# Softmax row sums in a two-layer hybrid trunk: one running sum with a split, or four partial sums in four quarters of the array

## The chip, the cores and the metric

The kernel runs on one core of one Trainium2 chip. The metric is the time of one execution on the device in microseconds (us). The program is one launch. TensorE (PE) multiplies, VectorE (DVE), ScalarE (ACT) and GpSimd (POOL) do the elementwise work, SyncE (SP) issues every DMA. Each engine takes its instructions in its own order and waits at an instruction until what it needs is there.

## The reference, cut to what matters

Two layers. Each has grouped-query attention and a gated linear recurrence side by side on the same normalised input. 1024 latent tokens and 256 context tokens; 16 query heads share 4 key heads of width 64. The part that matters here is the softmax:

```python
def gqa(q, k, v):
    s = jnp.einsum('bqkgd,bskd->bkgqs', q, k).astype(jnp.float32)
    p = jax.nn.softmax(s, axis=-1).astype(v.dtype)
    return jnp.einsum('bkgqs,bskd->bqkgd', p, v)
...
        o_lat = latent_attention(q_l, k_all, v_all)
...
        x = x + gt_l * merge_branches(o_lat, ga_l, lru_l, gb_l, gm_l, w_a_out[l], w_b_out[l], w_out[l])
```

Latent queries see 1280 keys (256 context, 1024 latent), context queries (first layer only) see the 256 context keys. All arithmetic is fp32 in the reference.

## The kernel before, in words

Features lie on the partitions, tokens on the free axis. To keep fp32 accuracy at the fast rate, the kernel writes an operand as a high and a low part in the type fp32r and adds three products (high·high, high·low, low·high).

A layer runs in four stages: queries, keys and values (line 709); the recurrence (766); attention, with the projections of the gates beside it (908); the output projections (1114). The change is in the third.

**Attention.** `Unit` (line 942) is 512 query columns of one head against ten tiles of 128 keys. A pair of heads has four units; in the first layer a fifth one (`e == 2`) takes the 256 context queries of both heads against two key tiles. The first layer has 32 full and 8 context units, the second 32 full ones. What a unit does, in the order of time:

- `load` (964): three DMAs bring the queries; POOL clears the lower half of `qb`.
- `s1` (977): twelve products give scores of 128 queries against up to 512 keys, and DVE takes their maxima into `mp`. `smax` and `aug` (984, 989): DVE reduces these to one maximum per query in column 64 of `mz`, PE transposes four 128x65 blocks, and ACT writes the negative maxima into row 64 of `qb`, so that the next product subtracts them.
- `s2` (996), for each key tile: two products give the shifted scores with keys on the partitions. ACT takes the exponential twice, as fp32 (`pf`) and as fp32r (`ph`). DVE subtracts: `pl` is the rest, pf − ph. `add` (1011): POOL adds `pf` to the running sum `acc`, nine additions for ten tiles.
- `av` (1020): two products with the values, one for `ph` and one for `pl`. `evac` (1028) brings the result out.
- `lparts` (1040): POOL copies `acc` to an fp32r tile `ah`, DVE subtracts to get the rest `al`. `lsum` (1046): two products with a column of ones add the 128 partitions of both into one row, ACT copies the row out, and a DMA writes it to memory.
- `recip` (1059), once for the two heads: a DMA brings the sums back as 128 partitions by 8, DVE takes reciprocals, a DMA writes them, two DMAs spread them over the partitions, and `done` (1080) scales the output.

**Order.** The class `Timeline` (63) keeps a clock of its own: each product adds a planned cost (`mm`, 135), and everything else is put into a list with a due time. The products of the gates' projections (`fills`, 901) fill the time between, and before each the due work is emitted. Within attention the due times are in steps of one key tile (lines 947 to 962), stretched by `pace` (1105), which is worked out from the planned costs. The order on PE is as emitted; the other engines' order is made from the emission by the tile framework. Tiles come from rings: three buffers of `pf`, two of `acc`, six PSUM banks for all scores and sums.

Of the kernel before, what the change touches and what calls it, by code (L numbers as in the profile page):

```python
# [62 lines left out]
class Timeline:  # L63
    """Orders the emission by the tensor engine's clock: products fill, other work is due at times."""
# [36 lines left out]
def trunk_kernel(ctx: ExitStack, tc: tile.TileContext, xT, cc, par, wmod, win, wgate, wo,  # L101
# [47 lines left out]
    # ---------------------------------------------------------------- constants  # L149
# [17 lines left out]
    ones_r = const.tile([128, 1], F32R, name="onesr")  # L167
    V.tensor_copy(ones_r, ones)
# [11 lines left out]
    # silu of the two conditions  # L180
# [10 lines left out]
    # 4 * softplus(-lam), by log1p(z) = 2 atanh(z / (2 + z)), z = exp(-|lam|)  # L191
# [27 lines left out]
    # ---------------------------------------------------------------- weights  # L219
# [53 lines left out]
    def w_next():  # L273
        """the next weight tile; the one after it is being made ready"""
# [26 lines left out]
    # ---------------------------------------------------------------- modulation  # L301
# [19 lines left out]
    def modulation(l, i, b, half, wm, box):  # L321
        """four feature tiles' part of 512 columns of shift | scale | gate, on the tensor engine"""
# [9 lines left out]
    def mod_turn(l, i, n, ps, wait):  # L332
        """two rows of sums to features on the partitions"""
# [12 lines left out]
    def modulation_side(l, blocks, work):  # L346
        """the same, its products beside the tensor engine"""
# [29 lines left out]
    # ---------------------------------------------------------------- hidden state  # L377
# [8 lines left out]
    def sq_add(work, c, j, x):  # L386
        """adds the squares of feature tile j of x"""
# [9 lines left out]
    def rsqrt_small(ss, scale, t):  # L397
        """t[:, 0] = 1 / sqrt(ss * scale + eps), with one Newton step"""
# [7 lines left out]
    def norm_chunk(l, c, xs, gap):  # L406
        """events that make the hidden state's two parts from xs [128, 8, n] and its squares"""
# [35 lines left out]
    # ---------------------------------------------------------------- queries and keys  # L443
# [8 lines left out]
    class Group:  # L452
        """two column tiles of queries or keys: product, per-head norm, rotation, two parts"""
# [22 lines left out]
        def sums(self, i, c, hi, lo):  # L476
            """sums of squares of the tile's two heads, in rows"""
# [12 lines left out]
        def norm(self, i):  # L490
            """their reciprocal roots, spread over all partitions"""
# [53 lines left out]
    def layer_dram(l):  # L545
# [7 lines left out]
        d["l"] = {(t, c): dtile(l, f"l{t}{c}", [2, 2, CH[c][1]]) for t in range(8) for c in och}  # L553
# [17 lines left out]
    def first_products(g):  # L571
        """the first group's products, with the last chunk of tokens last"""
# [11 lines left out]
    # ---------------------------------------------------------------- start  # L584
# [19 lines left out]
    with tc.tile_pool(name="prep", bufs=1, reuse_waits="tile") as work:  # L604
# [16 lines left out]
        def scale_rows(c):  # L621
            """x times the reciprocal root of its mean square, in its place"""
# [34 lines left out]
        def modulate(c, k0, nk=4):  # L657
            """the hidden state's two parts"""
# [44 lines left out]
    # ---------------------------------------------------------------- layers  # L703
    for l in range(DEPTH):
# [4 lines left out]
        # ---------------- queries, keys, values  # L709
# [169 lines left out]
            # the first of the gate projections cover the last scans  # L879
# [28 lines left out]
        # ---------------- attention, with the projections of the gates beside it  # L908
        use_banks("g")
        weng[0] = "a"  # L910
        with tc.tile_pool(name="att", bufs=2, reuse_waits="tile") as work:
            kv = {}

            def load_kv(g):
# [6 lines left out]
                G.memset(r32(k2[64:128]), 0.0)  # L921
# [4 lines left out]

            mzs = []
            for i in range(3):
# [160 lines left out]
            for t in range(8):  # L1089
                if t % 2 == 0:  # L1090
                    add(g0 - 19 if t else -25, lambda t=t: load_kv(t // 2))
                for c, e in [("L0", 0), ("L0", 1), ("L1", 0), ("L1", 1)] + ([] if last else [("C", 2)]):
# [5 lines left out]
                    if e:  # L1098
                        cost += 0.864 * CH[c][1] / 512
# [229 lines left out]
```

## Time and profile before

| | us |
|---|---|
| median of three runs (lowest, highest) | 3306.36 (3296.35, 3307.05) |
| span of the profiled execution, first to last instruction | 3297.0 |
| PE busy in the span | 3059.3 (93%) |
| DVE busy | 2656.1 (81%) |
| ACT busy | 1789.4 (54%) |
| POOL busy | 1435.6 (44%) |
| attention of the first layer, the stretch read below | 640 to 1380 |
| attention of the second layer, the stretch read below | 2340 to 3010 |

Of the profiled execution the page gives the span alone, so every sum is made against 3297.0; the median lies 9.4 us above it, and what a sum gives as a difference is applied to the median. Busy shares are averages over stages with different limits, so each stage has to be read by itself. A product's duration in the trace includes the time in which its results leave the array, and the next product starts before that: the distance of two starts tells the rate, not the duration.

### The profile page before, as it was taken

The numbers are of one execution on the slowest core, as the hardware profiler recorded it, in microseconds if no ns is written. First come the engines' busy times: TensorE is split into PE (matmuls) and PEld (weight loads), VectorE is DVE, ScalarE is ACT, GpSimd is POOL, SyncE is SP. The second block draws the span as 40 slices with busy tenths as digits, with TensorE's granted clock in tenths as the row PEclk, the third lists the DMA queues.
The fourth block names the chain that finished last, engine by engine and source line by source line (L and its number), as shares of the span: only waits on it lengthen the run. The fifth ranks groups of instructions, "written<-read, shape, count | busy, mean of one in ns | idle before, by whom it ended". The sixth has DMA issues, their size and how long they took to land.

```text
span 3297.0 us, 42932 instructions
## 1 busy us (share of the span) xinstructions
PE 3059.3 (93%) x14392; PEld 2437.3 (74%) x14392; DVE 2656.1 (81%) x3696; ACT 1789.4 (54%) x3140; POOL 1435.6 (44%) x1119
## 2 busy tenths in 40 slices
PE   7999999999989999999899999998998988899999
PEld 3778788777767677787777788776766666677887
DVE  7874887699999999766685876896899999997544
ACT  5433667366666666545655435665566666664222
POOL 0111443366667666435522212443577766773000
PEclk9999999999999999999999999999999999999999
DMA  5442111312112111264554451113212121114554
GB/s 196 145 162 91 48 50 63 112 52 69 59 61 78 54 58 61 86 196 154 177 198 157 144 179 48 52 48 94 83 50 60 54 71 52 52 53 139 195 177 138
DMA packets 218654, 331.14 MB, mean 100 GB/s; under 512 B 39184, under 2 KB 84904, under 8 KB 218176
## 3 DMA queue, kind: packets, MB, share of 16 engines
q1 hardware_dynamic: 218432, 328.39, 30.7%
q8 instruction: 113, 1.85, 0.2%
q14 instruction: 109, 0.89, 0.1%
HBM read 252.13 MB, written 76.17 MB: 100 GB/s over the span
## 4 chain that ended last, share of the span: by engine, by line
PE 43%; DVE 34%; issue 8%; POOL 6%; ACT 4%; DMA 4%; SPq 1%; DVEq 0%; POOLq 0%; ACTq 0%
PE gps L143 25%; DVE pl L1007 9%; DVE mp L982 6%; PE s2ps L143 4%; DVE wlo L227 4%; PE avps L143 4%; PE s1ps L143 2%; PE qps L143 2%; PE vps L143 2%; PE gtps L143 1%; DVE ti L851 1%; POOL macc L360 1%; POOL acc L1018 1%; POOL b L848 1%; DVE z L1085 1%
## 5 line engine op out<-in xcount | busy, mean ns | idle before, releaser
L143 PE MATMUL gps<-h,whi 128*128 128x512 f32 x3328 | 1042.7, 395 | 19.8 <-DVE g L871 14.5
L1018 POOL TENSOR_TENSOR acc<-acc,pf 128x512 f32<-128x512 f32 x512 | 745.4, 1456 | 339.9 <-ACT pf L1005 319.0
L1007 DVE TENSOR_TENSOR pl<-pf,ph 128x512 fp32r<-128x512 f32 x656 | 753.1, 1150 | 12.7 <-ACT ph L1006 10.3
L143 PEld LDWEIGHTS gps<-h,whi 128*128 128x128 f32 x3328 | 609.1, 189 | 145.4 <-issue 9.3
L143 PE MATMUL gps<-h,wlo 128*128 128x512 f32 x1664 | 654.5, 393 | 1.4 <-DVE wlo L227 1.4
L1005 ACT ACTIVATE pf<-s2ps 128x512 f32<-128x512 f32 x656 | 392.2, 598 | 382.4 <-issue 164.2
L982 DVE TENSOR_REDUCE mp<-s1ps 128x1 f32<-128x512 f32 (+1 forms) x800 | 450.5, 581 | 44.8 <-PE s1ps L143 43.5
L227 DVE TENSOR_TENSOR wlo<-wraw,whi 128x512 fp32r<-128x512 f32 x392 | 348.0, 910 | 80.6 <-POOL whi L224 43.1
L1006 ACT ACTIVATE ph<-s2ps 128x512 fp32r<-128x512 f32 x656 | 389.0, 593 | 0.0
L143 PEld LDWEIGHTS gps<-h,wlo 128*128 128x128 f32 x1664 | 314.8, 189 | 71.3 <-DVE wlo L227 2.1
L226 ACT ACTIVATE whi<-wraw 128x512 fp32r<-128x512 f32 x324 | 193.8, 628 | 304.4 <-PE gps L143 261.5
L143 PE MATMUL s1ps<-k,qa 128*128 128x512 f32 (+1 forms) x800 | 291.2, 372 | 58.1 <-DVE mp L982 37.1
L143 PE MATMUL avps<-pl,vv 128*128 128x512 f32 x656 | 266.7, 407 | 24.6 <-DVE pl L1007 23.0
L143 PE MATMUL s2ps<-qa,k 128*128 128x512 f32 x656 | 264.5, 403 | 18.2 <-DVE mp L982 15.9
L360 POOL TENSOR_TENSOR macc<-macc,wmt 128x512 f32<-128x512 f32 x112 | 155.8, 1391 | 250.9 <-ACT wmt L358 227.8
L143 PE MATMUL s2ps<-qb,k 128*128 128x512 f32 x656 | 259.5, 396 | 0.0
L143 PE MATMUL avps<-ph,vv 128*128 128x512 f32 x656 | 259.1, 395 | 0.0
L143 PE MATMUL gps<-e,whi 128*128 128x512 f32 x768 | 243.9, 399 | 0.2 <-DVE e L227 0.2
L143 PEld LDWEIGHTS s1ps<-k,qa 128*128 128x128 f32 x800 | 151.3, 190 | 116.4 <-DVE mp L982 63.4
L143 PE MATMUL qps<-h,whi 128*128 128x512 f32 x640 | 204.6, 401 | 1.7 <-DVE h L669 0.9
L143 PE MATMUL gps<-c,whi 128*128 128x256 f32 x1024 | 197.9, 288 | 2.3 <-DVE c L222 2.0
L527 POOL TENSOR_TENSOR t<-qg,rc 128x512 f32<-128x512 f32 x40 | 57.6, 1439 | 322.7 <-DVE qf L532 161.4
(225 smaller groups left out, 5325.0 us busy)
## 6 DMA issues: line engine op xcount, KB each, us to landing
wraw<-in_win_dram SPq DMA_DIRECT2D x200, 256.0 KB
wraw<-in_wo_dram SPq DMA_DIRECT2D x192, 256.0 KB
wm<-in_wmod_dram SPq DMA_DIRECT2D x32, 512.0 KB
wm<-in_wmod_dram SPq DMA_DIRECT2D x8, 1024.0 KB
rb<-rq SPq DMA_DIRECT2D x64, 128.0 KB
k<-k SPq DMA_DIRECT2D x24, 320.0 KB
v<-vst SPq DMA_DIRECT2D x20, 256.0 KB
vv<-v SPq DMA_DIRECT2D x8, 640.0 KB
```

The source lines that it names most:

```text
L143: nc.tensor.matmul(o, a, b, start=start, stop=stop)
L226: S.activation(dst_hi, src, AF.Copy)
L227: (V if lo_eng == "v" else G).tensor_sub(dst_lo, src, r32(dst_hi))
L360: G.tensor_add(acc, acc, t)
L527: G.tensor_mul(t1, a, rc[:, o:o + n])
L848: G.tensor_mul(a2, a2, ti)
L851: V.tensor_tensor_scan(h, a, a2, 0.0, op0=OP.mult, op1=OP.add)
L982: tl.at(0.3, lambda: V.reduce_max(self.mp[:, j, b:b + 1], ps[:, :n], axis=AX.X))
L1005: S.activation(pf, ps, AF.Exp)
L1006: S.activation(ph, ps, AF.Exp)
L1007: tl.at(1.4, lambda: V.tensor_sub(pl, pf, r32(ph)))
L1018: G.tensor_add(self.acc, self.acc, pf)
```

## The change

Four things change, all in attention.

1. The sums. A full unit keeps four partial sums, of the key tiles (0, 1, 2), (3, 4, 5), (6, 7) and (8, 9), a context unit two of one tile each. `lparts` goes: no `ah`, no `al`. `lsum` multiplies each partial sum, as it is in fp32, with a 128x32 block of ones, and each result goes to its own 32 partitions of one PSUM bank, so that each product stands in its own quarter of the array's columns. The plan counts 0.9 us for all of them.
2. The way back. The four rows of sums go to memory, `recip` brings them back with a DMA for each head, DVE adds the four and takes the reciprocal.
3. The maxima. `mz` is a 128x4 tile without the 64 cleared columns, the transposes put one row out each, and the second product of `s2` takes 65 rows instead of 128, so that `qb` and `k2` need no clearing.
4. The plan: `lsum` is due at 3.6 instead of 4.0 (5.0 instead of 6.0 for a context unit), `pace` follows the new costs. Comments and docstrings are taken out, so line numbers differ.

```diff
-    def mm(o, a, b, start, stop):
+    def mm(o, a, b, start, stop, cost=None):
...
-        if b.dtype == F32R:
+        if cost is not None:
+            tl.now += cost
+        elif b.dtype == F32R:
...
+    ones32 = const.tile([128, 32], F32, name="ones32")
+    V.memset(ones32, 1.0)
...
-                    add(g0 + self.nkt + (4.0 if e == 2 else 2.0), self.lparts)
-                    add(g0 + self.nkt + (6.0 if e == 2 else 4.0), self.lsum)
+                    add(g0 + self.nkt + (5.0 if e == 2 else 3.6), self.lsum)
+                    self.groups = ((0,), (1,)) if e == 2 else ((0, 1, 2), (3, 4, 5), (6, 7), (8, 9))
+                    self.accs = {}
...
-                    G.memset(r32(qb[64:128]), 0.0)
...
-                        tr(pt[0:65, j * 128:(j + 1) * 128], mz[:, j, :])
-                    S.activation(self.qb[64:65], pt[64:65, :], AF.Copy, scale=-1.0)
+                        tr(pt[0:1, j * 128:(j + 1) * 128], self.mz[:, j:j + 1])
+                    S.activation(self.qb[64:65], pt[0:1, :], AF.Copy, scale=-1.0)
...
-                    mm(ps, k2[:, ks], self.qb, False, True)
+                    mm(ps, k2[0:65, ks], self.qb[0:65], False, True)
...
                 def add(self, kt, pf):
-                    if kt == 0:
-                        self.first = pf
-                        self.acc = work.tile([128, 512], F32, name="acc", tag="acc", bufs=2)
-                    elif kt == 1:
-                        G.tensor_add(self.acc, self.first, pf)
+
+                    x = next(x for x, g in enumerate(self.groups) if kt in g)
+                    at = self.groups[x].index(kt)
+                    if at == 0:
+                        self.accs[x] = pf
+                        if self.e == 2:
+                            G.tensor_scalar(self.acc_tile(x), pf, 1.0, 0.0, op0=OP.mult, op1=OP.add)
+                    elif at == 1:
+                        first = self.accs[x]
+                        G.tensor_add(self.acc_tile(x), first, pf)
                     else:
-                        G.tensor_add(self.acc, self.acc, pf)
+                        G.tensor_add(self.accs[x], self.accs[x], pf)
+
+                def acc_tile(self, x):
+                    self.accs[x] = work.tile([128, 512], F32, name="acc", tag="acc", bufs=5)
+                    return self.accs[x]
...
-                def lparts(self):
-                    self.ah = work.tile([128, 512], F32R, name="ah", tag="ah", bufs=1)
-                    self.al = work.tile([128, 512], F32R, name="al", tag="al", bufs=1)
-                    G.tensor_scalar(self.ah, self.acc, 1.0, 0.0, op0=OP.mult, op1=OP.add)
-                    tl.at(1.5, lambda: V.tensor_sub(self.al, self.acc, r32(self.ah)))
-
                 def lsum(self):
-                    """sums of the exponentials over the keys, one row"""
+
                     lp = ptile("s", "lps")
-                    mm(lp[0:1], ones_r, self.ah, True, False)
-                    mm(lp[0:1], ones_r, self.al, False, True)
+                    ng = len(self.groups)
+                    for x in range(ng):
+                        mm(lp[32 * x:32 * x + 32], ones32, self.accs[x], True, True, 0.9 / ng)
...
+                        for e in range(2):
+                            DMA.dma_start(rs[64 * e:64 * e + 64], ls[e].rearrange("s (p x) -> p s x", p=64))
...
-                        V.reciprocal(rq, rq)
+                        r = rq[:, 32:32 + x]
+                        V.tensor_add(r, rs[:, 0], rs[:, 1])
+                        for y in range(2, ng):
+                            V.tensor_add(r, r, rs[:, y])
+                        V.reciprocal(r, r)
```

**PE, the sum of one unit in the middle of the first layer's attention.** `lps` is the bank of the sums, `gps` a gate's projection, `s1ps` and `s2ps` scores, `avps` the product with the values. Before:

```order
L143 MATMUL gps<-h_762,wlo 128x512
L143 MATMUL avps<-ph,vv 128x512
L143 MATMUL avps<-pl,vv 128x512
L143 MATMUL s1ps<-k_7302,qa 128x512
L143 MATMUL lps<-ah,onesr 1x512
L143 MATMUL lps<-al,onesr 1x512
L143 MATMUL s2ps<-qa,k_7302 128x512
L143 MATMUL s2ps<-qb,k_7303 128x512
L143 MATMUL s1ps<-k_7302,qa 128x512
L143 MATMUL avps<-ph,vv 128x512
```

And of the same unit now:

```order
L145 MATMUL gps<-h_802,whi 128x512
L145 MATMUL gps<-h_803,whi 128x512
L145 MATMUL gps<-h_802,wlo 128x512
L145 MATMUL lps<-acc,ones_91 32x512 x4
L145 MATMUL avps<-ph,vv 128x512
L145 MATMUL avps<-pl,vv 128x512
L145 MATMUL s1ps<-k_7336,qa 128x512
L145 MATMUL s2ps<-qa,k_7336 128x512
L145 MATMUL s2ps<-qb,k_7337 128x512
```

Two products of one row become four of 32 rows, at nearly the same place between the same neighbours; each of the four stands in its own 32 output partitions, and none waits for DVE any more.

**POOL, the end of a full unit and the context unit behind it.** Before (`ah` is the copy of the sum, the cleared `qb` belongs to a later unit):

```order
L1018 TENSOR_TENSOR acc<-acc,pf 128x512 x7
L967 MEMSET qb 64x512
L1018 TENSOR_TENSOR acc<-acc,pf 128x512
L1043 TENSOR_SCALAR ah<-acc 128x512
L967 MEMSET qb 64x512
L1016 TENSOR_TENSOR acc<-pf 128x512 x2
L1043 TENSOR_SCALAR ah<-acc 128x512
```

And now, where line 1013 copies a context unit's tile:

```order
L1016 TENSOR_TENSOR acc<-pf 128x512 x3
L1018 TENSOR_TENSOR acc<-acc,pf 128x512
L1016 TENSOR_TENSOR acc<-pf 128x512
L1018 TENSOR_TENSOR acc<-acc,pf 128x512
L1016 TENSOR_TENSOR acc<-pf 128x512 x2
L1013 TENSOR_SCALAR acc<-pf 128x512 x2
L1016 TENSOR_TENSOR acc<-pf 128x512
```

The run of seven additions is broken into ones and threes with pauses of one key tile between the groups, the copies and the clearing are gone, and the context unit has two copies in place of an addition and a copy.

**DVE, around the reciprocal of one pair of heads.** Before:

```order
L1007 TENSOR_TENSOR pl<-pf,ph 128x512
L987 TENSOR_REDUCE mz_5294<-mp 128x4
L1007 TENSOR_TENSOR pl<-pf,ph 128x512
L1069 RECIPROCAL rq<-rq 128x8
L1007 TENSOR_TENSOR pl<-pf,ph 128x512 x3
L1044 TENSOR_TENSOR al<-acc,ah 128x512
L982 TENSOR_REDUCE mp<-s1ps 128x1
L1007 TENSOR_TENSOR pl<-pf,ph 128x512 x2
```

And now:

```order
L1002 TENSOR_TENSOR pl<-pf,ph 128x512
L1074 TENSOR_TENSOR rq<-rq 128x8
L978 TENSOR_REDUCE mp<-s1ps 128x1
L1076 TENSOR_TENSOR rq<-rq 128x8
L1002 TENSOR_TENSOR pl<-pf,ph 128x512
L1076 TENSOR_TENSOR rq<-rq 128x8
L983 TENSOR_REDUCE mz<-mp 128x4
L1077 RECIPROCAL rq<-rq 128x8
L978 TENSOR_REDUCE mp<-s1ps 128x1
L1002 TENSOR_TENSOR pl<-pf,ph 128x512
```

The subtraction that made `al` is gone, and three additions of 128x8 stand ahead of the reciprocal (one of 128x4 for the context unit).

## Rows read from the trace of the kernel before

**Rows 1.** Busy time by stretch: PE, PEld, DVE, ACT, POOL, clock, DMA share, GB/s.

```profile
640.00:1380.00 740.00, 683.68 (x3199) 533.52 (x3198) 707.34 (x983) 470.92 (x882) 486.54 (x377) 1.00 0.19 61
...
2340.00:3010.00 670.00, 606.96 (x2593) 455.93 (x2592) 654.13 (x861) 426.45 (x790) 466.25 (x349) 0.99 0.18 57
...
3035.00:3297.00 262.00, 258.18 (x1123) 210.43 (x1122) 132.90 (x219) 62.50 (x106) 0.00 (x0) 1.00 0.54 177
```

**Rows 2.** Shares of the chain of waits, 640 to 1380 us.

```profile
by line: DVE pl L1007 15.6%; PE gps L143 15.4%; DVE mp L982 12.1%; PE s2ps L143 11.8%; PE avps L143 10.3%; issue 6.1%; PE s1ps L143 4.6%; DVE wlo L227 3.5%; POOL acc L1018 3.0%; DVE z L1085 2.4%; DVE al L1044 2.3%; DVE z L1038 2.1%; PE mtps
```

**Rows 3.** Shares of the chain of waits, 2340 to 3010 us.

```profile
by line: DVE pl L1007 25.0%; DVE mp L982 14.9%; PE gps L143 10.6%; issue 8.8%; PE avps L143 8.3%; PE s2ps L143 7.6%; PE s1ps L143 4.0%; DVE wlo L227 3.7%; POOL acc L1018 2.5%; DVE z L1038 2.0%; DVE z L1085 1.9%; DVE rl L1083 1.9%; DVE al L1
```

**Rows 4.** VectorE by line, 640 to 1380 us: count | busy us, mean ns | idle before.

```profile
L1007 DVE TENSOR_TENSOR pl<-pf,ph 128x512 fp32r<-128x512 f32 x336 | 387.6, 1155 | 10.5 <-ACT ph L1006 9.2
...
L1044 DVE TENSOR_TENSOR al<-acc,ah 128x512 fp32r<-128x512 f32 x40 | 36.1, 903 | 11.4 <-POOL ah L1043 11.4
...
L1069 DVE RECIPROCAL rq<-rq 128x8 f32<-128x8 f32 (+1 forms) x23 | 4.2, 181 | 1.7 <-DMA rq<-l7L 1.7
```

**Rows 5.** VectorE by line, 2340 to 3010 us.

```profile
L1007 DVE TENSOR_TENSOR pl<-pf,ph 128x512 fp32r<-128x512 f32 x315 | 360.0, 1145 | 1.6 <-ACT ph L1006 0.5
...
L1044 DVE TENSOR_TENSOR al<-acc,ah 128x512 fp32r<-128x512 f32 x32 | 34.3, 1072 | 4.5 <-POOL ah L1043 4.5
```

**Rows 6.** One tile, pl: shortest, median and longest duration in ns.

```profile
L1007 DVE TENSOR_TENSOR pl<-pf,ph x656: 670/1174/1823, 639.4 to 2998.3; 128x512 fp32r<-128x512 f32 x164
```

**Rows 7.** Order of time around one sum: start us, duration us, engine.

```profile
1013.40 0.40 PE L143 MATMUL avps<-pl,vv 128*128 128x512 f32 x1
...
1013.63 0.39 PE L143 MATMUL lps<-ah,onesr 128*1 128x512 f32 x1
1013.70 1.29 POOL L1018 TENSOR_TENSOR acc<-acc,pf 128x512 f32<-128x512 f32 x1 [0.38 <-ACT pf L1005]
1013.79 1.75 DVE L1044 TENSOR_TENSOR al<-acc,ah 128x512 fp32r<-128x512 f32 x1
...
1015.59 0.39 PE L143 MATMUL lps<-al,onesr 128*1 128x512 f32 x1 [1.57 <-DVE al L1044]
...
1015.82 0.39 PE L143 MATMUL s2ps<-qa,k 128*128 128x512 f32 x1
```

**Rows 8.** GpSimd by line, 640 to 1380 us.

```profile
L1018 POOL TENSOR_TENSOR acc<-acc,pf 128x512 f32<-128x512 f32 x256 | 366.0, 1430 | 186.6 <-ACT pf L1005 179.1 <-DVE mz L987 0.3 <-POOL ah L1043 0.3
...
L1016 POOL TENSOR_TENSOR acc<-pf 128x512 f32<-128x512 f32 x40 | 58.7, 1469 | 82.8 <-ACT pf L1005 81.5 <-PE gps L143 1.1
...
L1043 POOL TENSOR_SCALAR ah<-acc 128x512 fp32r<-128x512 f32 x40 | 38.2, 954 | 6.3 <-issue 3.5
```

**Rows 9.** GpSimd by line, 2340 to 3010 us.

```profile
L1018 POOL TENSOR_TENSOR acc<-acc,pf 128x512 f32<-128x512 f32 x253 | 375.6, 1484 | 151.3 <-ACT pf L1005 137.9 <-PE mtps L147 4.7 <-PE avps L143 0.8
...
L1016 POOL TENSOR_TENSOR acc<-pf 128x512 f32<-128x512 f32 x31 | 43.3, 1396 | 32.1 <-ACT pf L1005 32.1
...
L1043 POOL TENSOR_SCALAR ah<-acc 128x512 fp32r<-128x512 f32 x32 | 29.2, 911 | 2.8
```

**Rows 10.** TensorE by line and shape, 640 to 1380 us: the narrow products.

```profile
L143 PE MATMUL gps<-c,whi 128*128 128x256 f32 x272 | 53.0, 284 | 0.0
L143 PE MATMUL s1ps<-k,qa 128*128 128x256 f32 x155 | 44.4, 294 | 10.2 <-DVE ga L897 6.0 <-DVE mp L982 4.2
L143 PE MATMUL gps<-c,wlo 128*128 128x256 f32 x136 | 38.2, 281 | 0.0
L147 PE MATMUL mtps<-ident,mz 128*65 128x128 f32 x156 | 23.4, 272 | 0.0
```

**Rows 11.** TensorE by line and shape, 2340 to 3010 us: the narrow scores.

```profile
L143 PE MATMUL s1ps<-k,qa 128*128 128x256 f32 x120 | 34.8, 290 | 5.8 <-DVE mp L982 4.7 <-DVE ga L897 0.9
```

**Rows 12.** One tile, modps: shortest, median and longest duration in ns.

```profile
L143 PE MATMUL modps<-wm,cs x64: 591/592/1057, 7.1 to 49.2; 128*2 128x512 f32 x64
```

**Rows 13.** Order of time on TensorE, ten of these one behind the other.

```profile
45.37 4.45 PE L143 MATMUL modps<-wm,cs 128*2 128x512 f32 x10
```

More of the change, by code (lines that the diff above doesn't have):

```diff
@@ L166, in trunk_kernel @@
     V.tensor_copy(sel_r, sel)
-    ones_r = const.tile([128, 1], F32R, name="onesr")
-    V.tensor_copy(ones_r, ones)
+    ones32 = const.tile([128, 32], F32, name="ones32")
+    V.memset(ones32, 1.0)
     ident = const.tile([128, 128], F32, name="ident")
@@ L552, in layer_dram @@
         d["za"] = {(t, c): dtile(l, f"za{t}{c}", [128, CH[c][1]]) for t in range(8) for c in och}
-        d["l"] = {(t, c): dtile(l, f"l{t}{c}", [2, 2, CH[c][1]]) for t in range(8) for c in och}
+        d["ls"] = {(t, c): dtile(l, f"ls{t}{c}", [4, 512] if c == "C" else [2, 4, 512]) for t in range(8) for c in och}
+        d["l"] = {(t, c): dtile(l, f"l{t}{c}", [2, CH[c][1]]) for t in range(8) for c in och}
         d["gm"] = {(t, c): dtile(l, f"gm{t}{c}", [128, CH[c][1]]) for t in range(16) for c in och}
@@ L925, in load_kv @@
                 kv[g] = k1, k2, v
-            mzs = []
-            for i in range(3):
-                mz = work.tile([128, 4, 65], F32, name=f"mz{i}", bufs=1)
-                G.memset(mz, 0.0)
-                mzs.append(mz)
             ev = []
@@ L984, in smax @@
                 def smax(self):
-                    mz = mzs[self.i % 3]
                     nb = 1 if self.e == 2 else 3
-                    V.reduce_max(mz[:, :, 64], self.mp[:, :, :nb], axis=AX.X)
+                    self.mz = work.tile([128, 4], F32, name="mz", tag="mz", bufs=3)
+                    V.reduce_max(self.mz, self.mp[:, :, :nb], axis=AX.X)
                 def aug(self):
-                    mz = mzs[self.i % 3]
                     pt = ptile("s", "mtps")
                     for j in range(4):
-                        tr(pt[0:65, j * 128:(j + 1) * 128], mz[:, j, :])
-                    S.activation(self.qb[64:65], pt[64:65, :], AF.Copy, scale=-1.0)
+                        tr(pt[0:1, j * 128:(j + 1) * 128], self.mz[:, j:j + 1])
+                    S.activation(self.qb[64:65], pt[0:1, :], AF.Copy, scale=-1.0)
                 def s2(self, kt):
@@ L1061, in recip @@
                     n = CH[self.c][1]
-                    ld = dd["l"][self.t, self.c]
-                    flat = [ld[i].rearrange("e (p x) -> (e p) x", p=64) for i in range(2)]
-                    rq = const.tile([128, 8], F32, name="rq", tag="rq", bufs=2)[:, 0:n // 64]
-                    DMA.dma_start(rq, flat[0])
+                    ls, ld = dd["ls"][self.t, self.c], dd["l"][self.t, self.c]
+                    ng, x = len(self.groups), n // 64
+                    rq = const.tile([128, 40], F32, name="rq", tag="rq", bufs=2)
+                    rs = rq[:, 0:ng * x].rearrange("p (s x) -> p s x", s=ng)
+                    if self.e == 2:
+                        DMA.dma_start(rs, ls[0:ng].rearrange("s (p x) -> p s x", p=128))
+                    else:
+                        for e in range(2):
+                            DMA.dma_start(rs[64 * e:64 * e + 64], ls[e].rearrange("s (p x) -> p s x", p=64))
                     rl = sm("rl")
                     def back():
-                        V.reciprocal(rq, rq)
-                        tl.at(0.5, lambda: DMA.dma_start(flat[1], rq), True)
+                        r = rq[:, 32:32 + x]
[3 more added lines that the diff above has]
+                        V.reciprocal(r, r)
+                        tl.at(0.5, lambda: DMA.dma_start(ld.rearrange("e (p x) -> (e p) x", p=64), r), True)
                         tl.at(4.0, spread, True)
@@ L1096, in trunk_kernel @@
                     g0 += 2 if ctxu else 10
-                    cost += (4 * 0.108 + 2 * 0.864 + 0.45 if ctxu else 4 * 0.54 + 10 * 0.864 + 0.45)
-                    if e:
-                        cost += 0.864 * CH[c][1] / 512
+                    cost += (4 * 0.108 + 2 * 0.864 + 1.34 if ctxu else 4 * 0.54 + 10 * 0.864 + 1.34)
             ev.sort(key=lambda x: (x[0], x[1]))
```

11 lines of the change are left out of this document (5 added, 6 removed).

## The prediction

> **What bounds the kernel now.** I first cut the span into stages by the table of windows, since the page's shares (PE 93%, DVE 81%) average over stages with different limits. Outside attention nothing of substance changes, so the two stretches of attention are read alone. In the first DVE works 707.3 of 740 us (96%) and in the second 654.1 of 670 us (98%), PE 92% and 91% by records whose ends are modelled [rows 1]. In the last stretch of the program, where nothing but PE limits, PE shows 258.18 of 262 us, 98.5% [rows 1]; attention does not reach that. What PE needs is better read from starts: one product of 512 columns follows the other at 0.23 us (1013.40 to 1013.63, and 1015.59 to 1015.82) [rows 7]. Of the 3199 records of the first stretch 272 + 155 + 136 + 156 = 719 are narrow, 256 or 128 columns [rows 10]; I take 0.115 us for those. 2480 x 0.23 + 719 x 0.115 = 653 us, 88% of the stretch. In the second, 120 narrow scores [rows 11] and four transposes for each of 31 units make 244 of 2593: 2349 x 0.23 + 244 x 0.115 = 568 us, 85%. So PE has 87 and 102 us to spare and DVE 33 and 16. The chain of waits agrees: DVE's `pl` alone holds 15.6% and 25.0% of it, the maxima 12.1% and 14.9%, and PE's products stand between them [rows 2, 3]. DVE bounds attention, and PE, which takes its work in order, stands still whenever a tile from DVE is late. The granted clock is 1.00 and 0.99 in both, the upper of its two levels (2.4 GHz) [rows 1], and does not enter the sum.
>
> Why DVE is so full shows in one tile: `pl`, a subtraction of two tiles in SBUF, takes 0.670 us at the shortest, 1.174 at the median, 1.823 at the longest [rows 6]. In the order of time, DVE's `al` starts at 1013.79, 0.09 us behind a POOL addition of 1.29 us, and takes 1.75; it ends about 0.55 us after POOL does [rows 7]. A DVE instruction of this kind that meets a POOL addition waits it out.
>
> **The change part by part.**
>
> *DVE, removed.* All `al`: 40 x 0.903 = 36.1 us and 32 x 1.072 = 34.3 us [rows 4, 5].
>
> *DVE, relieved.* `pl` costs 336 x (1.155 − 0.670) = 163 us and 315 x (1.145 − 0.670) = 150 us more than at its shortest [rows 4 to 6]. POOL's adding and copying goes from 366.0 + 58.7 + 38.2 = 462.9 us [rows 8] to 32 x 6 = 192 additions x 1.435 (the mean of the first two rows) and 16 copies x 0.954: 291 us, 37% less. In the second layer 375.6 + 43.3 + 29.2 = 448.1 us [rows 9] become 192 x 1.475 = 283 us, also 37% less. I take the extra time of `pl` to fall in that ratio: −60 and −55 us. Ends: nothing, if the additions that stay are those that collide; 48%, if a tile without an addition of its own (four of ten) never collides and the rest gain a little. The 37% is the share by time, between them.
>
> *DVE, added.* Three additions of 128x8 for each pair of full units, one for a pair of context heads: 56 and 48. The nearest row is the reciprocal of the same shape, 0.181 us [rows 4]: +10 and +9. Meeting POOL each might cost up to 0.49 more, `pl`'s mean stretch: +27 and +24 as the upper end. They wait for two DMAs in place of one; behind them on DVE stand `pl` and the maxima, for which PE waits. Today that wait is 1.7 us in 23 reciprocals [rows 4], and a landing 2 us later at each of 40 would take 80 us out of the slack that DVE gains below, so I count nothing and keep it for the range.
>
> DVE then needs 707 − 36 − 60 + 10 = 621 and 654 − 34 − 55 + 9 = 574 us.
>
> *PE, removed.* The two products of a sum, 0.46 us each unit: 653 − 18 = 635 and 568 − 15 = 553 us.
>
> *PE, added.* Four true fp32 products of 512 columns (two in a context unit). One such product, `modps`, is two records: 32 in the program, 64 in the trace [rows 12]; ten records take 4.45 us [rows 13], 0.43 each when about 0.16 for the last one's way out is set aside. No row shows two products in different quarters of the array. The lower end is that all four run beside each other and take the time of one, 2 x 0.43 = 0.86 us. The upper end is one behind the other, 3.44. Between them lies a third order: PE starts its work in the program's order, and the two records of a product use the same quarter, so the second waits for the first; only then the next product's first record can start, beside it. That makes five steps of 0.43, 2.15 us (three, 1.29, for a context unit). It is also the middle of the two ends, and I take it. PE's need: 635 + 32 x 2.15 + 8 x 1.29 = 714 us, and 553 + 32 x 2.15 = 622 us.
>
> A page speaks against the placing: the Trainium skill (TensorEngine Tiling (Array Packing), Key Properties) says that a change of the tiling mode drains TensorE. The sum of before has one column of ones and follows a full-width product at 0.23 us, and is followed by one at 0.23 us [rows 7], the distance of equal neighbours, so the trace shows no drain worth a term; with a drain as long as a product's way out (0.16) at two changes in 72 units the sum would be 23 us worse.
>
> *Cover that goes or comes.* The transposes put one row out instead of 65; their stationary side gets shorter, their 128 columns do not, so 156 records at 0.272 [rows 10] stay as they are. The cleared halves of `qb` lie on POOL beside other work: nothing. ACT reads 128 rows of sums instead of one, of equal length: nothing. `pf` has three buffers, and a group's first tile is now held until the next tile's addition, one tile longer than before in three places of ten; POOL, lighter by 37%, is never as late as it is now, so nothing.
>
> **The sum.** DVE at 621 and 574 us falls below PE at 714 and 622, so PE is late next. A stretch ends at what its fullest engine needs over the share that this engine reaches: DVE reaches 0.96 and 0.98 today, PE 0.985 where it is alone. I take 0.97: 714/0.97 = 736 and 622/0.97 = 641 us, −4 and −29. Together −33 us on 3297.0; the median of 3306.36 becomes 3273, and I say 3270. At 0.98 or 0.96 it would be 14 us less or more, and with `pl` not relieved at all DVE would need 681 and 629, which leaves the first layer as it is and takes the second to about 648.
>
> **The rivals.**
>
> *All four beside each other.* PE needs 635 + 40 x 0.86 = 669 and 553 + 28 = 581; DVE at 621 and 574 is close behind. 669/0.97 = 690 and 581/0.97 = 599: −121 us, 3185. For it: the four products share neither output partitions nor columns, and wait for nothing of each other. Against it: two records for each product in a queue that starts in order. A page says this outright: the Trainium skill (TensorEngine Tiling (Array Packing), Key Properties) has tiles as independent and lets different tiles execute loads and products in parallel. By that rule this rival would be the forecast; no row here shows it for fp32.
>
> *One behind the other, slower than before.* If quarters do not overlap in fp32, a full unit's sum holds PE for 3.44 us, between the products of the neighbouring unit. PE needs 635 + 110 + 14 = 759 and 553 + 110 = 663: 782 and 684 us, +56, 3362. It decides from about 2.6 us for the four on: there (635 + 36 x 2.6 + 553 + 32 x 2.6)/0.97 is the 1410 us of today. For it: every fp32 product in the trace stands behind the one before it [rows 13]. Against it: those all use the same quarter.
>
> *The transposes lose their one pass.* Their output now takes one quarter. If they ran as ordinary fp32 products, two records of 128 columns (0.43/4 each) in place of one, four in 72 units would cost 4 x 0.107 x 72 = 31 us on PE, and 3273 becomes 3304, no change. Beside it stands a page: the Trainium skill (TensorEngine Tiling (Array Packing), Restrictions) lists transposes of fp32 operands as incompatible with column tiling. No row of before has a transpose in a quarter.
>
> *The relief does not come,* because the additions that stay are those that meet `pl`: DVE 681 and 629, PE 714 and 622; −4 and −22, 3280, inside the forecast's own range.
>
> **How the numbers follow.** The forecast, with the relief in any size: 0.42, its own range 3245 to 3295. All four abreast: 0.28. One behind the other: 0.20. The transposes: 0.06. Late DMAs in front of the new additions, which eat the gain: 0.04. A measurement of this kernel can tell about 0.3%, 10 us, from no change. Faster: 0.28 from the first rival and 0.37 of the forecast's 0.42, 0.65. No change: the rest of the forecast, the transposes and half of the late DMAs, 0.13 with a little from the serial case between its ends. Slower: 0.22. The range of 8 in 10 reaches half-way into the first rival's lower side and over most of the serial case: 3178 to 3360.
>
> **What would show it.** In the stretches of attention DVE's busy share falls to about 85 to 90% and PE's rises; `pl`'s mean falls from 1.155 and 1.145 to about 0.98; POOL's busy time falls by about 37%, in both. The eight records of a full unit's sum span 2.15 us from the first start to the next product; a span of 0.9 makes the first rival true and 3.4 the second. Two records for a transpose in place of one show the third. If DVE stays over 95% busy, the reading of its collisions with POOL is wrong.

## The result, and the profile after

The changed kernel takes 3215.55 us (median of four runs, 3212.85 to 3225.26) against 3305.77 for the kernel before on the same chip: ratio 0.9741, 95% interval 0.9725 to 0.9757. That is 90 us less by the medians and 86 by the ratio. The forecast was 3270, 36 us less; the measured time lies inside the range, nearer to the first rival (3185) than to the forecast.

The profiled execution spans 3210.9 us, 86 us less than before. From the first second-score product (`s2ps`) to the last product with the values (`avps`), counted from start to start, attention went from 734.4 to 702.1 us in the first layer and from 673.5 to 623.6 us in the second: 82 of the 86 us. Where the other 4 come from was not followed.

The table of windows over both stretches of attention, with the columns of [rows 1]:

```profile
640.00:1345.00 705.00, 692.61 (x3398) 530.16 (x3396) 615.23 (x994) 471.19 (x878) 276.66 (x210) 1.00 0.21 64
2303.00:2920.00 617.00, 602.65 (x2765) 455.62 (x2764) 572.93 (x874) 426.05 (x786) 267.10 (x191) 0.99 0.20 61
```

PE is now busy 98% of both. DVE is busy 87% and 93%, where it was 96% and 98% [rows 1]. The granted clock is 1.00 and 0.99, as before. The chain of waits in the same two stretches, in that order:

```profile
by line: PE gps L145 26.9%; PE avps L145 17.9%; PE s2ps L145 17.1%; PE s1ps L145 7.7%; DVE mp L978 6.4%; DVE pl L1002 5.4%; PE lps L145 4.7%; issue 3.9%; PE mtps L149 2.2%; DVE wlo L229 1.5%; DVE rl L1091 1.0%; DVE z L1093 0.9%; DVE z L1042
by line: PE gps L145 24.8%; PE avps L145 21.3%; PE s2ps L145 20.1%; PE s1ps L145 9.4%; DVE pl L1002 5.6%; PE lps L145 4.5%; DVE mp L978 4.3%; issue 2.5%; PE mtps L149 2.0%; DVE wlo L229 1.5%; DVE z L1093 0.9%; DVE rl L1091 0.6%; ACT pf L100
```

`pl` held 15.6% and 25.0% of it before [rows 2, 3] and holds 5.4% and 5.6% now; PE's products lead. The new sums, `lps`, hold 4.7% and 4.5%.

DVE by line in the first stretch (count | busy us, mean ns | idle before), then the tile `pl` in the whole run, shortest, median and longest duration in ns:

```profile
L1002 DVE TENSOR_TENSOR pl<-pf,ph 128x512 fp32r<-128x512 f32 x336 | 319.1, 950 | 59.6 <-ACT ph L1001 57.9
L978 DVE TENSOR_REDUCE mp<-s1ps 128x1 f32<-128x512 f32 (+1 forms) x400 | 222.2, 576 | 14.0 <-PE s1ps L145 12.6
...
L229 DVE TENSOR_TENSOR wlo<-wraw,whi 128x512 fp32r<-128x512 f32 x32 | 24.8, 803 | 1.1 <-ACT whi L228 1.1
...
L1076 DVE TENSOR_TENSOR rq<-rq 128x8 f32<-128x8 f32 x31 | 9.2, 297 | 0.7
...
L1074 DVE TENSOR_TENSOR rq<-rq 128x8 f32<-128x8 f32 (+1 forms) x23 | 3.6, 155 | 2.1 <-DMA rq<-ls7L 2.1
```

```profile
L1002 DVE TENSOR_TENSOR pl<-pf,ph x656: 639/693/1791, 640.7 to 2912.1; 128x512 fp32r<-128x512 f32 x164
```

`pl`'s mean fell from 1155 to 950 ns, its median from 1174 [rows 6] to 693, so that half of them now take about as long as one that meets no addition (0.68 us). DVE sits idle 57.9 us before them, waiting for ScalarE, where it was 9.2 [rows 4]. GpSimd by line in the first stretch:

```profile
L1016 POOL TENSOR_TENSOR acc<-pf 128x512 f32<-128x512 f32 x128 | 174.5, 1364 | 365.4 <-ACT pf L1000 365.4
L1018 POOL TENSOR_TENSOR acc<-acc,pf 128x512 f32<-128x512 f32 x64 | 89.1, 1392 | 40.0 <-ACT pf L1000 38.5 <-POOL acc L1016 0.4
L1013 POOL TENSOR_SCALAR acc<-pf 128x512 f32<-128x512 f32 x16 | 11.0, 685 | 53.7 <-PE lps L145 48.7 <-ACT pf L1000 5.0
```

Together they take 274.6 us where there were 462.9 [rows 8].

Now the sums. TensorE in order of time around one full unit's sum (start us, duration us):

```profile
1015.66 0.39 PE L145 MATMUL s2ps<-qb,k 65*128 65x512 f32 x1
1015.89 0.28 PE L145 MATMUL s1ps<-k,qa 128*128 128x256 f32 x1
1016.10 1.06 PE L145 MATMUL lps<-acc,ones 128*32 128x512 f32 x8
1017.10 0.51 PE L145 MATMUL avps<-ph,vv 128*128 128x512 f32 x1
1017.44 0.39 PE L145 MATMUL avps<-pl,vv 128*128 128x512 f32 x1
```

The four products' eight records take 1.00 us from their first start (1016.10) to the next product's start (1017.10), not 2.15. Two edges come to it. The 256-column product ahead lasts 0.21 us to the next start, 0.09 more than the 0.115 such a product needs; the one behind lasts 0.34 (1017.10 to 1017.44) in place of 0.23, 0.11 more. In all that is 1.2 us. The tile `lps` in the stretch from 1016.12 to 1016.50, and from 1016.60 to 1017.09:

```profile
L145 PE MATMUL lps<-acc,ones x4: 617/617/617, 1016.1 to 1016.1; 128*32 128x512 f32 x4
```

```profile
L145 PE MATMUL lps<-acc,ones x8: 592/604/617, 1016.1 to 1016.6; 128*32 128x512 f32 x8
```

At 1016.12 four records are already under way and until 1016.50 no fifth begins; the other four come at about 1016.6. So all four first passes (a product is two records; they are called its two passes here) start together, 6 to 7 ns apart when read record by record, then all four second passes, 0.45 us behind them. And the transposes, the tile `mtps`:

```profile
L149 PE MATMUL mtps<-ident,mz x288: 269/272/275, 634.2 to 2890.2; 128*1 128x128 f32 x144
```

Each is still one record, 272 ns as before [rows 10]. What PE waits for in the first stretch (in all us, times, longest us), now and then before:

```profile
PE mtps L149 <- DVE mz L983: 5.3, 6, 1.2
PE lps L145 <- DVE mp L978: 4.1, 5, 1.2
PE s2ps L145 <- DVE mp L978: 1.6, 3, 0.6
```

```profile
PE s1ps L143 <- DVE mp L982: 17.7, 23, 1.6
PE lps L143 <- DVE al L1044: 16.1, 11, 1.7
PE s2ps L143 <- DVE mp L982: 10.1, 11, 1.7
```

The waits of the scores for the maxima are nearly gone, and the wait of `lps` for `al` is gone with `al`.

### The profile page after: what moved, and what is told of

It reads as the page before. It is cut to its first block, busy times and chain, and to the rows that moved or that the text cites. A ratio compares the mean times of both kernels' runs of the same rounds, so it can differ in the third digit from the quotient of the medians.

```text
span 3210.9 us, 42915 instructions
## 1 busy us (share of the span) xinstructions
PE 3061.0 (95%) x14792; PEld 2429.0 (76%) x14792; DVE 2484.4 (77%) x3728; ACT 1793.6 (56%) x3140; POOL 1016.7 (32%) x777
## 4 chain that ended last, share of the span: by engine, by line
PE 60%; DVE 21%; issue 7%; ACT 4%; DMA 4%; POOL 3%; SPq 1%; DVEq 0%; POOLq 0%; ACTq 0%
PE gps L145 32%; PE avps L145 8%; PE s2ps L145 8%; PE s1ps L145 4%; DVE wlo L229 3%; DVE pl L1002 2%; DVE mp L978 2%; PE qps L145 2%; PE lps L145 2%; PE vps L145 2%; POOL macc L362 1%; DVE ti L854 1%; PE gtps L145 1%; DMA rb<-rq 1%; POOL b L851 1%
## 5 line engine op out<-in xcount | busy, mean ns | idle before, releaser
L1002 DVE TENSOR_TENSOR pl<-pf,ph 128x512 fp32r<-128x512 f32 x656 | 629.7, 960 | 83.3 <-ACT ph L1001 79.8
L1016 POOL TENSOR_TENSOR acc<-pf 128x512 f32<-128x512 f32 x256 | 350.8, 1370 | 713.8 <-ACT pf L1000 712.2
L229 DVE TENSOR_TENSOR wlo<-wraw,whi 128x512 fp32r<-128x512 f32 x392 | 333.3, 873 | 77.0 <-POOL whi L226 40.1
L145 PE MATMUL avps<-ph,vv 128*128 128x512 f32 x656 | 266.7, 407 | 0.0
L145 PE MATMUL s2ps<-qb,k 65*128 65x512 f32 x656 | 260.5, 397 | 0.0
L1018 POOL TENSOR_TENSOR acc<-acc,pf 128x512 f32<-128x512 f32 x128 | 181.9, 1421 | 71.0 <-ACT pf L1000 68.9
```

What stands on the lines that cost most here:

```text
L229: (V if lo_eng == "v" else G).tensor_sub(dst_lo, src, r32(dst_hi))
L1002: tl.at(1.4, lambda: V.tensor_sub(pl, pf, r32(ph)))
L1016: G.tensor_add(self.acc_tile(x), first, pf)
L1018: G.tensor_add(self.accs[x], self.accs[x], pf)
```

## The experiments

Ten kernels were run, every ratio against the kernel before on the same chip; the code is shown in short form. The theory: TensorE runs a product in each quarter of the array at the same time, so the sums cost it one product's time and not five steps; and the larger part of the gain is the relief of `pl`. The rivals: the products take turns by the order in which they stand; or the gain comes from `al` and PE alone. The fourth part of the change, the plan, was not run by itself, so its share is not known.

### One quarter for all four products

```diff
-  mm(lp[32 * x:32 * x + 32], ones32, accs[x], True, True)
+  mm(lp[0:32], ones32, accs[x], x == 0, x == ng - 1)
```

> The four products of a unit's sum all in the first quarter of the array, one accumulating on the other; one row of sums comes back, so the small additions on VectorE go. Theory (the quarters run beside each other, each with its own line of records, and PE now bounds attention): eight records of 0.43 us in one line, 3.44 us from the first start to the last end, some 3.7 with what stands around it, against 1.2 with four quarters. PE needs 32 x 2.5 + 8 x 0.8 = 86 us more in the first layer and 80 in the second, and nearly all of it shows: about 3375 us. Rival (VectorE still sets the pace of attention, PE has room): most of it is hidden, under 3260 us.

Measured 3359.52 us, ratio 1.0159 (1.0141 to 1.0177): slower than before, and 15 us under the theory's 3375. TensorE in order of time around a full unit's sum:

```profile
1027.24 3.62 PE L145 MATMUL lps<-acc,ones 128*32 128x512 f32 x8
1030.79 0.50 PE L145 MATMUL avps<-ph,vv 128*128 128x512 f32 x1
1031.13 0.39 PE L145 MATMUL avps<-pl,vv 128*128 128x512 f32 x1
```

The same eight records take 3.55 us in one quarter. The placing is worth 2.55 us a unit and 144 us of the run, although this kernel also does without the small additions on DVE. The serial rival of the prediction (3362 us) is this kernel.

### Two quarters, in two orders

```diff
-  mm(lp[32 * x:32 * x + 32], ones32, accs[x], True, True)
+  y = (0, 1, 0, 1)[x]        # the second kernel: (0, 0, 1, 1)
+  mm(lp[32 * y:32 * y + 32], ones32, accs[x], first in y, last in y)
```

> The same four products in two quarters, in the order first, second, first, second. Own line for each quarter: four records one behind the other in each, 1.72 us and some 0.3 around it, 0.85 more than with four quarters in each of 64 full units: 54 us, about 3270. Strict order of starts (the rule of the prediction: no record starts before the one ahead of it in the program, and a product's two records follow each other): five steps of 0.43, 2.15 and 0.3 around, about 3295.

> The same four products in two quarters, in the order first, first, second, second. Own line for each quarter: as with the alternating order, 1.72 us and some 0.3, about 3270 and equal to it. Strict order of starts: the second quarter's first record starts beside the first quarter's last one, seven steps of 0.43, 3.0 us and 0.3, about 3350, some 55 us above the alternating order.

Measured 3249.33 us, ratio 0.9827 (0.9812 to 0.9842), with the quarters in turn, and 3248.29, 0.9826 (0.9808 to 0.9844), with two in a row in each. TensorE around a sum, in turn and then in a row:

```profile
1023.62 1.91 PE L145 MATMUL lps<-acc,ones 128*32 128x512 f32 x8
1025.46 0.50 PE L145 MATMUL avps<-ph,vv 128*128 128x512 f32 x1
```

```profile
1024.90 1.92 PE L145 MATMUL lps<-acc,ones 128*32 128x512 f32 x8
1026.75 0.50 PE L145 MATMUL avps<-ph,vv 128*128 128x512 f32 x1
```

They take 1.84 and 1.85 us. By the order that the prediction assumed, (0, 0, 1, 1) would have to hold the second pair back behind the first. It does not. Read record by record, the second record starts 7 ns behind the first with the quarters in turn and 13 ns with two in a row, where the second product cannot have begun, since two records of one quarter lie at least 0.43 us apart in the kernel with one quarter; so the third product starts before the second. Each quarter has its own line, and the longest line sets the time (3.55, 1.84, 1.00 us for four, two and one product in a quarter). The rival of turns by order falls. The times are some 21 us under the theory's 3270: 0.84 us more in each of 64 units is 54 us of PE's work, of which 34 show.

### One running sum, one product

```diff
-  groups = ((0, 1, 2), (3, 4, 5), (6, 7), (8, 9))
+  groups = (tuple(range(10)),)
```

> One running sum per unit as before (nine additions on GpSimd), no split, one fp32 product with ones in one quarter. Theory (the relief of VectorE comes in two parts: its own subtraction gone, and less waiting for GpSimd): only the first part comes; VectorE needs 707 - 36 = 671 and 654 - 34 = 620 us and stays over 93% busy, pl stays at a mean of about 1.13 us, PE needs 635 + 34 = 669 and 581: about 3235 us, 20 above the four partial sums. Rival (the subtraction alone was what bound): as fast as the four partial sums or faster by the PE time saved, 3200 us or less.

Measured 3257.44 us, ratio 0.9856 (0.9839 to 0.9874). TensorE around its sum, and the window of the first stretch:

```profile
1021.93 1.04 PE L145 MATMUL lps<-acc,ones 128*32 128x512 f32 x2
1022.91 0.51 PE L145 MATMUL avps<-ph,vv 128*128 128x512 f32 x1
```

```profile
640.00:1345.00 705.00, 678.82 (x3108) 514.77 (x3107) 658.70 (x931) 463.35 (x864) 410.29 (x295) 1.00 0.21 63
```

A single product takes 0.98 us: in the changed kernel the other three are all but free. PE's work is the same, `al` is gone here too, yet it is 42 us slower than the changed kernel. The difference is GpSimd, 410.3 us of the window against 276.7, and `pl` with it (mean 1117 and 1163 ns in the two layers against 950 and 971). It came out 22 us slower than the theory's number, so the relief is worth more than I had by then. It also splits the gain: 47 us of it come here, with `al`, the third part and the plan, and the other 42 with the partial sums. Taken last, the relief is thus about half of the gain and not clearly the larger part.

### The relief alone, and the relief taken back

The first kernel is the one before with three of the nine additions left out (key tiles 3, 6 and 8 are not in the sums, and the row of sums is copied out with 1 added). The second is the changed kernel with three additions more (the first tile of three groups is added to itself, so that it counts twice).

```diff
 the kernel before:
-  else:
+  elif kt not in (3, 6, 8):
       G.tensor_add(self.acc, self.acc, pf)
 the changed kernel:
   self.accs[x] = pf
+  if self.e != 2 and kt in (0, 6, 8):
+      G.tensor_add(self.acc_tile(x), pf, pf)
```

> The kernel before with three of the nine additions of a unit left out on GpSimd (key tiles 3, 6 and 8 are missing in the sums; the row of sums is copied out with 1 added, so that none is zero). The split and its subtraction stay. Theory (VectorE waits for GpSimd's additions): pl's mean falls from 1.15 to about 0.97, VectorE needs 60 and 55 us less, 647 and 599, PE as before 653 and 568: about 3215 us, or 90 faster than before. Rival (the subtraction and its chain were the bound): within 20 us of before.

> The changed kernel with nine additions on GpSimd in place of six: at the start of three of the four groups the tile is added to itself, so its exponentials count twice in the sums. Theory: pl's mean goes back from 0.96 to about 1.1 us, VectorE needs about 50 us more in each layer (668 and 617): about 3245 us, 30 above the changed kernel. Rival (PE bounds and VectorE has room enough): within 8 us of the changed kernel.

Measured 3231.14 us, ratio 0.9790 (0.9775 to 0.9804), and 3256.22, ratio 0.9869 (0.9853 to 0.9886). Window and `pl` (count | busy us, mean ns) of the first stretch, three left out:

```profile
640.00:1345.00 705.00, 675.41 (x3195) 533.69 (x3194) 637.11 (x980) 472.60 (x880) 347.79 (x281) 1.00 0.21 64
```

```profile
L1007 DVE TENSOR_TENSOR pl<-pf,ph 128x512 fp32r<-128x512 f32 x335 | 331.3, 990 | 40.0 <-ACT ph L1006 38.8
```

and three put back into the changed kernel:

```profile
640.00:1345.00 705.00, 678.38 (x3297) 513.92 (x3296) 648.49 (x981) 462.67 (x862) 387.14 (x301) 1.00 0.21 63
```

```profile
L1002 DVE TENSOR_TENSOR pl<-pf,ph 128x512 fp32r<-128x512 f32 x330 | 326.9, 992 | 36.2 <-ACT ph L1001 34.8
...
L229 DVE TENSOR_TENSOR wlo<-wraw,whi 128x512 fp32r<-128x512 f32 x32 | 31.6, 1017 | 0.0
...
L1078 DVE TENSOR_TENSOR rq<-rq 128x8 f32<-128x8 f32 x30 | 15.1, 502 | 0.7
```

Three additions fewer give 70 us where 90 were expected; three more in the changed kernel cost 41 where 30 were expected. The rival, that the relief is worth little, falls on both sides. The second kernel shows that the size depends on what else is there to be hit. Its `pl` takes 992 ns in the first stretch against 950 in the changed kernel (1062 against 971 in the second layer; about 1.1 us had been expected in both), but the weights' `wlo` and the additions of `rq` grow more (1017 and 502 ns against 803 and 297). GpSimd's additions stretch whatever DVE reads from two tiles in SBUF at that moment. They do not stretch the rest: the maxima `mp`, which DVE reads from PSUM, take 576 ns in the changed kernel, and in the kernel before, over the same window,

```profile
L982 DVE TENSOR_REDUCE mp<-s1ps 128x1 f32<-128x512 f32 (+1 forms) x395 | 218.5, 575 | 2.0 <-PE s1ps L143 1.3
```

### The third part alone, and the memsets put back

The first kernel is the one before with only the maxima in four columns, the one-row transposes, the 65 rows and the memsets gone. The second is that one with the memset of `qb`'s second half, partitions 64 to 127, back, the third the changed kernel with it.

```diff
 the kernel before:
-  G.memset(r32(qb[64:128]), 0.0)
-  tr(pt[0:65, ...], mz[:, j, :])
+  tr(pt[0:1, ...], self.mz[:, j:j + 1])
-  mm(ps, k2[:, ks], self.qb, False, True)
+  mm(ps, k2[0:65, ks], self.qb[0:65], False, True)
 the second and the third:
   qb = self.qb = work.tile([128, 512], F32R, ...)
+  G.memset(r32(qb[64:128]), 0.0)
```

> The kernel before with the third part of the change alone: maxima without the cleared columns, transposes with one output row, 65 rows in the second score product, no clearing of qb and k2. Theory: nothing of it is on the path, within 8 us of before; GpSimd loses some 40 us of clearing, which writes and does not read. Rival: the clearing too holds VectorE up, then 10 to 25 us faster.

> The kernel before with the third part of the change alone (maxima in four columns, transposes that put out one row, 65 rows in the second score product), but with the clearing of qb's upper half for every unit put back on GpSimd (72 memsets of 0.52 us). Theory: the 18 us that the third part gave by itself come from these memsets, which stand in GpSimd's queue ahead of the next unit's first addition and shift the additions onto pl; then the time goes back to that of the kernel before, 3300 us within 6, and pl's mean in the first stretch goes from 1.114 back to about 1.15. Rival: they come from the shorter rows and another order; then it stays near 3283 us, pl near 1.115.

> The changed kernel with the same 72 memsets of qb's upper half put back on GpSimd. Theory: in the changed kernel TensorE is busy 98% of attention and VectorE 87 to 93%, so what the memsets cost VectorE is hidden, and the time stays within 6 us of the changed kernel (3216). Rival: they cost the same 18 us as in the kernel before, 3234.

Measured: the third part alone 3282.64 us, ratio 0.9944 (0.9927 to 0.9962); with the memset back 3299.36, 0.9987 (0.9976 to 0.9999); the changed kernel with the memset 3218.73, 0.9750 (0.9734 to 0.9766). The part that I had counted as nothing gives 18 us by itself, the rival of its first expectation. By the two ratios some 14 of these 18 us are the memset's, give or take 7: 72 instructions of half a microsecond on an engine that is busy two thirds of the time. GpSimd's row for it in the second kernel, 640 to 1380 us:

```profile
L960 POOL MEMSET qb<- 64x512 f32 x37 | 19.3, 521 | 6.6 <-POOL ah L1035 4.8
```

DVE by line from 640 to 1345 us, without the memset and with it:

```profile
L998 DVE TENSOR_TENSOR pl<-pf,ph 128x512 fp32r<-128x512 f32 x330 | 365.8, 1109 | 10.7 <-ACT ph L997 9.2
...
L227 DVE TENSOR_TENSOR wlo<-wraw,whi 128x512 fp32r<-128x512 f32 x32 | 27.6, 881 | 0.0
```

```profile
L999 DVE TENSOR_TENSOR pl<-pf,ph 128x512 fp32r<-128x512 f32 x324 | 363.5, 1123 | 11.5 <-ACT ph L998 10.3
...
L227 DVE TENSOR_TENSOR wlo<-wraw,whi 128x512 fp32r<-128x512 f32 x32 | 32.1, 1020 | 0.0
```

`pl` goes back by only a part of what I expected in the first layer (1114 to 1129 ns, not 1150) and by more in the second (1141 to 1165 ns); `wlo` by 0.14 us each in the first. Over both layers that is 13 us of `pl`, most of the loss. A memset alone does not stretch `pl`: seven in the trace of before that met nothing else took 0.683 us. So it is likely to act by moving the additions behind it in GpSimd's queue onto other DVE work; which, one by one, was not settled, and the way is argued, not shown. In the changed kernel the same memsets cost 3 us, no more than the intervals leave open (0.9750 beside 0.9741), as the theory had it. Its first window:

```profile
640.00:1345.00 705.00, 691.91 (x3392) 528.94 (x3391) 620.22 (x993) 471.88 (x880) 297.27 (x247) 1.00 0.22 65
```

DVE shows 620.2 in place of 615.2 us and still has 85 us of the window to spare.

### Two partial sums a unit, one set of products a pair of heads

```diff
-  groups = ((0, 1, 2), (3, 4, 5), (6, 7), (8, 9))
+  groups = ((0, 1, 2, 3, 4), (5, 6, 7, 8, 9))
-  four products in each unit
+  four products in every second unit, for both heads of the pair
```

> A candidate: two partial sums for each unit (eight additions) and one set of four products for the two heads of a pair, each in its own quarter. PE spends 1.2 us for two units in place of 2.4: 19 us less in each layer; VectorE waits more for GpSimd, about 25 us in each layer, and is at 646 and 599 us against PE's 664 and 572. If PE bounds both layers as the trace says, about 3190; if VectorE is close enough behind to take it back, 3215 or more.

Measured 3229.50 us, ratio 0.9786 (0.9772 to 0.9801); the second of the two expected times. Its window of the first stretch:

```profile
640.00:1345.00 705.00, 678.88 (x3245) 523.31 (x3247) 643.66 (x959) 458.42 (x859) 376.49 (x273) 1.00 0.20 64
```

It halves the sums on PE, but has eight additions a unit in place of six: GpSimd 376.5 us, DVE 643.7, `pl` 1023 ns in that stretch. What PE saves comes back as DVE's waiting for GpSimd. No version that was run is faster than the changed kernel.

## Why the prediction was right in direction and too small

**What bounded it, and how DVE is relieved: right.** DVE's need was put at 621 and 574 us; the windows show 615.2 and 572.9, a busy share of 93% in the second, over the 85 to 90% that the prediction named. `al` is gone. `pl` was forecast at a mean of about 0.98 us and came to 0.950 and 0.971; relief −69 us in the first layer, 336 x (1.155 − 0.950), where −60 was expected, and −55 in the second, as expected. GpSimd's time fell by 41% in the first layer, not 37%, since an addition took 1.37 us there and not 1.435. Counted record by record, 583 of 656 `pl` overlapped an addition or a copy before, mean 1.209 us, and 382 do now, mean 1.160; those that overlap none take 0.68 in both. The small additions cost 12.8 us in the first stretch for the 10 forecast, and wait 2.1 us for their DMAs: no late DMAs.

**The failed step: the price of the four products.** "PE starts its work in the program's order, and the two records of a product use the same quarter, so the second waits for the first; only then the next product's first record can start, beside it. That makes five steps of 0.43, 2.15 us". The trace has 1.00 us and 1.2 with its edges. The second pass of a product does not hold back the next product in another quarter: four first passes have started by 1016.12, and (0, 1, 0, 1) costs what (0, 0, 1, 1) does. I had taken the middle of two ends, 0.86 and 3.44, with a story for it; the lower end was the truth but for the edges. What I had cited for the rival, the Trainium skill (TensorEngine Tiling (Array Packing), Key Properties), says that tiles are independent, and the runs agree: 3.55, 1.84, 1.00 us.

The edges, 0.09 us ahead and 0.11 behind, are a second, smaller term that I had put at nothing. The first rival left them out too, with 0.14 us of the product's own time, and for that came out some 25 us too low. Whether they are the drain at a change of mode that the Trainium skill states (same section) is not shown: a product behind the four transposes of the kernel before, 65 rows each and so in no quarter, also takes 0.32 us (1020.26 to 1020.58) in place of 0.23.

```profile
1019.90 0.60 PE L147 MATMUL mtps<-ident,mz 128*65 128x128 f32 x4
1020.26 0.48 PE L143 MATMUL s1ps<-k,qa 128*128 128x512 f32 x1
1020.58 0.39 PE L143 MATMUL avps<-ph,vv 128*128 128x512 f32 x1
```

The one column of [rows 7], from which I had read that there is no edge, was an fp32r product; the four of the change are plain fp32.

With 1.2 us in place of 2.15 (1.29 for a context unit) the prediction's own formula gives PE 635 + 40 x 1.2 = 683 and 553 + 32 x 1.2 = 591 us; divided by 0.97, 704 and 610, against 702.1 and 623.6 measured. The share of 0.97 holds in the first layer (683/702.1 = 0.973). In the second it is 0.948, where DVE is busy 93%. Two quarters, heavier on PE, reach 0.986 and one quarter 0.989 in the first layer (635 + 32 x (1.84 + 0.2) + 8 x 1.18 = 710 of 720.2; 635 + 32 x 3.75 + 8 x 2.03 = 771 of 779.6). The share of the fullest engine is thus no constant: here it is lower where the second engine comes near.

**What followed from it.** Since PE was thought to be late next, the relief looked as if it hardly mattered ("The relief does not come", 3280, 10 us from the forecast). In truth three additions a unit are worth 41 us of the changed kernel's time.

**The third part, counted as nothing.** "The cleared halves of `qb` lie on POOL beside other work: nothing." Alone it gave 18 us. Work on POOL was not beside other work, it was in the way of it; "nothing" holds only in the changed kernel (3 us), where DVE has room. I had priced an edit as hidden by an engine that I had just named as the cause of the stall.

**The rivals.** All four beside each other: right in mechanism. One behind the other: true of one quarter only. That 3359.52 was measured there for the 3362 worked out is in part luck: a sum cost 3.75 us and not 3.44, and PE reached a share of 0.989 in the first layer and not 0.97. The transposes keep one record of 272 ns. Of the restriction on transposes that the Trainium skill states (TensorEngine Tiling (Array Packing), Restrictions) no effect is seen here.

## What to carry to other kernels

When a price lies between "side by side" and "one behind the other", do not take the middle: decide what resource the pieces share, and let the chance stand on the two ends. Before an edit is costed at nothing because it is hidden, ask whether the engine that hides it is the one that others wait for; and when the bound moves to another engine, work out again what every other edit is then worth.

## What the runs showed of the hardware

- Products of fp32 into different 32-column quarters overlap almost completely: one product alone takes 0.98 us from its start to the next product's, four in four quarters 1.00, two in each of two 1.84, four in one 3.55. The order in which they stand makes no difference (1.84 and 1.85). The Trainium skill (TensorE: Matmul & The Clock Gate, Part 3: Packing small matmuls — row/col tiling) says that products start and end strictly in order. These fp32 products do not keep to that: with two in a row in each quarter, the third starts 13 ns behind the first, ahead of the second.
- Around plain fp32 products in quarters, between full-width fp32r products, PE loses 0.09 us ahead and 0.11 us behind. Which of the two changes costs it is open.
- A DVE subtraction of two SBUF tiles that starts while a GpSimd addition runs ends 0.55 us after that addition (0.546 to 0.553 between the 10th and 90th percentile of 486 `pl` of the kernel before), however long it had been waiting. It is not slowed, it waits. Where it is the addition that starts inside `pl`, `pl` keeps its 0.68 us, and an addition that starts inside such a subtraction takes 1.54 us on average against 1.35 for the others: the one that comes second waits. The Trainium skill (SBUF — State Buffer, SBUF: two separate sides) calls this an exclusive lock, for a DVE operation with two inputs in SBUF against a GpSimd operation that reads SBUF. Both halves agree: a memset, which reads nothing, left `pl` at 0.683 us, and `mp`, which reads PSUM, takes 0.68 us for 512 columns whether an addition runs at its start or not.
